# Layer 1's two attentions: negated scaled queries, softmax by head, grouped latent norms and another background plan

## The chip, the core and the metric

The kernel runs on one core of one Trainium2 chip. The metric is the time of one execution on the device, in microseconds (us), as the median of some runs. One profiled execution of the kernel before gives the trace that is read here. Its engines are named as in the profile: PE is TensorE's matmul, PEld its loading of weights, DVE is VectorE, ACT is ScalarE, POOL is GpSimd and SP is SyncE, which issues the DMAs.

## What is computed

A trunk of two transformer layers over 512 tokens (an 8 x 64 grid) with 256 context tokens beside them, 1024 features, all in float32. Layer 0 mixes with a pooling and a grouped attention; layer 1 with two attentions whose outputs are joined: MLA (8 heads, queries and keys from latents, 96 features a head, over all 768 keys) and a neighbourhood attention (8 heads of 64 features, 8 x 16 windows of the grid with a bias, and the 256 context keys). Each layer ends with a SwiGLU. Cut to the part that matters:

```python
def rmsnorm(x, g):
    xf = x.astype(jnp.float32)
    y = xf * lax.rsqrt(jnp.mean(xf * xf, axis=-1, keepdims=True) + EPS)
    return y.astype(x.dtype) * g

...
    def mla_q(cq_, T):
        q_ = (rmsnorm(cq_, q_a_gain) @ w_uq).reshape(B, T, MLA_HEADS, MLA_QK)
        return rmsnorm(q_, mla_q_gain)

    def mla_kv(ckv_, kr_, T):
        kv = (rmsnorm(ckv_, kv_a_gain) @ w_ukv).reshape(B, T, MLA_HEADS, MLA_NOPE + MLA_V)
        k_rope = jnp.broadcast_to(kr_[:, :, None, :], (B, T, MLA_HEADS, MLA_ROPE))
        k_ = jnp.concatenate([kv[..., :MLA_NOPE], k_rope], axis=-1)
        return rmsnorm(k_, mla_k_gain), kv[..., MLA_NOPE:]
    ...
    o_mla = block_attention(mq[:, :, :, None], jnp.concatenate([mkc, mk], axis=1),
                            jnp.concatenate([mvc, mv], axis=1), mla_scale).reshape(B, S, MLA_HEADS * MLA_V)
    ...
    na_scale = NA_HEAD_DIM ** -0.5
    o_na = neighbourhood_attention(q_na, k_na, v_na, k_nac, v_nac, na_rpb, na_scale).reshape(B, S, NA_DIM)

    out = jnp.concatenate([o_mla, o_na], axis=-1) @ w_out
```

## The kernel before

Activations are kept with features on the partitions and tokens along the free dimension. A float32 value is split into a high and a low part in the fp32r type (`H` and `L`), and a product is made of two or three matmuls (`mm3`, lines 133 to 137). Weights are loaded by SP into a staging buffer `wraw` (tag `wr`, four buffers), cast to `wH` on ACT (L123), and `wL` is the remainder, subtracted on DVE or POOL (L124).

The two attentions of layer 1 are 32 steps, driven by `paired`. First come 16 steps of window attention (`na_units`: 4 pairs of heads x 4 blocks of 128 queries), then 16 steps of MLA (`mla_units`: 4 pairs of heads x 4 blocks of queries). Each step has three parts. `scores` makes the scores in PSUM, the softmax's maximum on DVE (window: L1208 over the 256 context keys of both heads, then L1210, which adds the bias and takes the maximum over the window; MLA: L373), the bias `nb` of the exponential (L375), the exponential on ACT (L378), the reciprocal of its sum on DVE (L380) and the normalisation on POOL (L382). `turn` transposes the probabilities on PE (L389) into one of two PSUM buffers `ps_tp`, and copies them out on ACT (L165) or DVE (L167). `values` multiplies them with V (L1226, L1266). A step's `turn` runs one step after its scores, its `values` two steps after. Of a window step, all of `turn` comes at the end of the next step; of an MLA step two of its three transposes come right after the next scores.

Between them runs the background: the latents' queries, keys and values for MLA, which the plans `na_plan` and `mla_plan` deal out to the 32 steps. A `make` is a matmul of a latent with its weights into PSUM, a copy and a square on ACT (L1087, L1088), a sum on DVE (L1091) and then the inverse square root `rsqrt` without a table: eleven DVE instructions on 4 or 8 columns (L238, L244, and three times L247, L248, L249). Products with it follow: for queries on DVE (L1138, L1139), a rotation on POOL (L318 to L320) and its sum (L322); for keys on DVE (L1109) and POOL (L1111). A background `turn` (`turn_pair`, L1080) transposes two heads into a `ps_tp` buffer and splits them out, alternately on ACT (L344, `mQH`, `mKH`) and DVE (L345, `mQL`, `mKL`). The `make` of a value copies from PSUM on ACT (L1156). Keys that are made wait for their turns in staging buffers of the weights (tag `wr`), three for each of two groups of heads.

PE's order is written out: `block` in `paired` puts each part behind PE's last instruction. The order of the other engines' queues is chosen by the framework's scheduler, which may also bring loads forward as far as buffers allow. Each engine runs its queue in order.

## Time and profile before

| | us |
|---|---|
| median of three runs | 1744.32 (1743.94 to 1746.56) |
| the profiled execution | 1746.14 |
| its span in the trace | 1744.3 |
| PE busy | 1660.2 (95%) |
| DVE busy | 948.5 (54%) |
| ACT busy | 637.1 (37%) |
| POOL busy | 260.0 (15%) |

The span runs from the first to the last instruction that the profiler saw. A busy time is a sum over stages that have different limits, and the ends of PE's matmuls are modelled, so its 95% does not say that nothing can be won; what stops the kernel is read stage by stage. The span's stretches are named by us from its start. A wait is named by what ended it, an inference from semaphores.

### The profile page before, as it was taken

To read this page: it belongs to the slowest core of one execution; us is meant where nothing else is said; L and a number is where in the kernel's file an instruction comes from. 1 tells how busy PE (TensorE), PEld (TensorE's weight loads), DVE (VectorE), ACT (ScalarE), POOL (GpSimd) and SP (SyncE) were. 2 spreads that over 40 slices of the span, in tenths; PEclk is the share of its full clock that TensorE was granted. 3 is DMA by queue.
4 is the path that set the end of the run, shared out by engine and by line. 5 is a ranking of instruction groups with operands and counts; after the bars stand their busy time and mean duration, and the time that the engine had idled before them with its cause. 6 is when DMAs were issued, how large, how long until landed. Compare 5 with 4: busy or idle time off the path is not lost.

```text
span 1744.3 us, 29055 instructions
## 1 busy us (share of the span) xinstructions
PE 1660.2 (95%) x11662; PEld 1475.7 (85%) x11662; DVE 948.5 (54%) x2052; ACT 637.1 (37%) x1241; POOL 260.0 (15%) x406
## 2 busy tenths in 40 slices
PE   6898999999999999999999999879789999999999
PEld 3687777798888888888889999768678998999897
DVE  5687667555945434523327973867665543333332
ACT  4453556534211221121224643555554432232231
POOL 1441333110000000000001202645330100000000
PEclk8899999999999999999999999989999999999999
DMA  8311334301625414512213213210203032222221
GB/s 286 149 34 53 145 131 173 133 26 65 208 96 187 151 55 153 167 61 67 73 61 110 76 50 96 73 36 28 83 13 134 34 112 98 85 97 97 97 76 58
DMA packets 61527, 171.25 MB, mean 98 GB/s; under 512 B 7248, under 2 KB 15440, under 8 KB 61392
## 3 DMA queue, kind: packets, MB, share of 16 engines
q1 hardware_dynamic: 61392, 169.39, 28.8%
q8 instruction: 92, 1.51, 0.3%
q14 instruction: 43, 0.35, 0.1%
HBM read 160.05 MB, written 4.19 MB: 94 GB/s over the span
## 4 chain that ended last, share of the span: by engine, by line
PE 84%; DVE 8%; ACT 3%; DMA 2%; issue 1%; POOL 1%; SPq 0%; ACTq 0%; DVEq 0%; POOLq 0%
PE ps_one L135 17%; PE ps_one L136 17%; PE ps_one L137 17%; PE ps_tp L137 5%; PE ps_tp L135 5%; PE ps_tp L136 5%; PE ps_tp L389 3%; PE ps_pv L777 2%; ACT prob L378 1%; PE ps_pv L135 1%; PE ps_pv L137 1%; PE ps_pv L136 1%; PE ps_big L135 1%; PE ps_big L137 1%; PE ps_big L136 1%
## 5 line engine op out<-in xcount | busy, mean ns | idle before, releaser
L123 ACT CAST wH<-wraw 128x1024 fp32r<-128x1024 f32 (+5 forms) x215 | 195.0, 915 | 404.9 <-PE ps_one L136 199.4
L124 DVE TENSOR_TENSOR wL<-wraw,wH 128x1024 fp32r<-128x1024 f32 (+3 forms) x191 | 219.6, 1155 | 169.4 <-ACT wH L123 167.2
L137 PE MATMUL ps_one<-hH,wL 128*128 128x512 f32 (+1 forms) x704 | 236.8, 336 | 0.0
L136 PE MATMUL ps_one<-hL,wH 128*128 128x512 f32 (+1 forms) x704 | 236.8, 336 | 0.0
L135 PE MATMUL ps_one<-hH,wH 128*128 128x512 f32 (+1 forms) x704 | 236.7, 336 | 0.0
L137 PE MATMUL ps_tp<-hH,wL 128*128 128x256 f32 x704 | 196.6, 280 | 0.0
L136 PE MATMUL ps_tp<-hL,wH 128*128 128x256 f32 x704 | 196.3, 279 | 0.0
L135 PE MATMUL ps_tp<-hH,wH 128*128 128x256 f32 x704 | 196.0, 280 | 0.0
L137 PE MATMUL ps_one<-aH,wL 128*128 128x512 f32 (+1 forms) x560 | 194.0, 347 | 0.0
L136 PE MATMUL ps_one<-aL,wH 128*128 128x512 f32 (+1 forms) x560 | 193.9, 347 | 0.0
L135 PE MATMUL ps_one<-aH,wH 128*128 128x512 f32 (+1 forms) x560 | 193.5, 347 | 0.0
L289 POOL TENSOR_SCALAR hH<-nt 128x256 fp32r<-128x256 f32 (+1 forms) x72 | 39.5, 557 | 735.3 <-ACT nt L288 733.3
L137 PEld LDWEIGHTS ps_one<-hH,wL 128*128 128x128 f32 x704 | 132.2, 188 | 15.4
L136 PEld LDWEIGHTS ps_one<-hL,wH 128*128 128x128 f32 x704 | 132.2, 188 | 14.4
L135 PEld LDWEIGHTS ps_one<-hH,wH 128*128 128x128 f32 x704 | 132.3, 188 | 14.1
L382 POOL TENSOR_SCALAR prob<-prob,rs 128x768 f32<-128x768 f32 (+2 forms) x136 | 107.2, 798 | 198.4 <-DVE rs L380 136.3
L135 PEld LDWEIGHTS ps_tp<-hH,wH 128*128 128x128 f32 x704 | 132.3, 188 | 0.9
L136 PEld LDWEIGHTS ps_tp<-hL,wH 128*128 128x128 f32 x704 | 132.0, 188 | 1.0
L137 PEld LDWEIGHTS ps_tp<-hH,wL 128*128 128x128 f32 x704 | 132.3, 188 | 0.1
L389 PE MATMUL ps_tp<-ident,prob 128*128 128x128 f32 x656 | 98.9, 285 | 22.4 <-DVE mQL L345 5.9
L135 PEld LDWEIGHTS ps_one<-aH,wH 128*128 128x128 f32 x560 | 105.8, 189 | 14.7
L136 PEld LDWEIGHTS ps_one<-aL,wH 128*128 128x128 f32 x560 | 105.6, 189 | 14.6
(303 smaller groups left out, 3541.8 us busy)
## 6 DMA issues: line engine op xcount, KB each, us to landing
wraw<-in_ada_dram SPq DMA_DIRECT2D x80, 512.0 KB, 3.8
wraw<-in_wg_dram SPq DMA_DIRECT2D x44, 512.0 KB, 3.5
wraw<-in_wu_dram SPq DMA_DIRECT2D x44, 512.0 KB, 3.5
wraw<-in_wd_dram SPq DMA_DIRECT2D x32, 384.0 KB, 3.0
wraw<-in_wd_dram SPq DMA_DIRECT2D x16, 512.0 KB, 3.5
wraw<-in_w1n_dram SPq DMA_DIRECT2D x12, 512.0 KB, 3.5
adaw<-in_adaq_dram SPq DMA_DIRECT2D x16, 256.0 KB, 5.4
wraw<-in_adaq_dram SPq DMA_DIRECT2D x8, 512.0 KB, 6.2
```

The lines of the kernel that those rows point to most:

```text
L123: act.copy(H, raw[:, :cols])
L124: eng.tensor_tensor(L, raw[:, :cols], H.bitcast(F32), op=ALU.subtract)
L135: pe.matmul(o, aH, bH, start=first, stop=False)
L136: pe.matmul(o, aH, bL, start=False, stop=False)
L137: return pe.matmul(o, aL, bH, start=False, stop=last)
L289: last = (pool.tensor_scalar(H, t[:, :n], 1.0, 1.0, op0=ALU.mult, op1=ALU.mult), sub(L, t[:, :n], H))
L378: act.activation(pr[i], S[:, i, :], AF.Exp, bias=nb[:, i:i + 1], scale=scale, accum_out=sm[:, i:i + 1])
L382: pool.tensor_scalar(pr[i], pr[i], r[:, i:i + 1], 1.0, op0=ALU.mult, op1=ALU.mult)
L389: pe.transpose(tp[:, 128 * i:128 * i + 128], b, ident)
L777: pe.matmul(st["pv"][64 * hd:64 * hd + 64, tq], V[kt][:, 64 * kv:64 * kv + 64], pt[:, hd, kt - k0, :], start=kt == k0, stop=kt == 5)
```

## The change

Six things, all in layer 1's attentions.

1. The gains of the queries are multiplied by minus the softmax's scale (`neg`, two DVE instructions), so the scores come out scaled and negated. The row's minimum is then the exponential's bias as it stands: `softmax_of_negated` computes exp(mn - S) and has no L375. The window's bias is multiplied by -1 instead of by 8 on POOL.
2. In the window attention each head has its own minimum, exponential, reciprocal and normalisation, right behind its own four matmuls, the context keys first. Before, L1208, L375 and L380 were made for both heads at once.
3. All copies of the window's transposed probabilities go to ACT; before, two of three did.
4. The inverse square roots of the latents' norms are grouped: one for the four tiles of a pair of query heads (8 columns) instead of two of 4 columns, one for the six tiles of a group of key heads (24 columns) instead of three of 8. The products that follow go with it.
5. In a window step, background transposes are put right behind the scores, ahead of the values and of the makes.
6. The plan deals the background out anew: a step has a pair of lists, transposes and makes. The queries of the last two pairs of heads and the second group of keys move by one to three steps, loads of their weights by up to four.

```diff
     def rsqrt(r, src, scale, table=True):
         n = r.shape[-1]
-        m = small.tile([P, 8], F32, tag="nwm", name="nwm")[:, :n]
-        t = small.tile([P, 8], F32, tag="nwt", name="nwt")[:, :n]
+        width, tag, bufs = (8, "", 8) if n <= 8 else (24, "k", 1)
+        m = small.tile([P, width], F32, tag="nwm" + tag, name="nwm", bufs=bufs)[:, :n]
+        t = small.tile([P, width], F32, tag="nwt" + tag, name="nwt", bufs=bufs)[:, :n]
...
+    def softmax_of_negated(S, pr, mn):
+        sm = small.tile([P, 2], F32, tag="sm", name="sm")
+        act.activation(pr, S, AF.Exp, bias=mn, scale=-1.0, accum_out=sm[:, 0:1])
+        r = small.tile([P, 2], F32, tag="rs", name="rs")
+        dve.reciprocal(r[:, 0:1], sm[:, 0:1])
+        pool.tensor_scalar(pr, pr, r[:, 0:1], 1.0, op0=ALU.mult, op1=ALU.mult)
...
             early = turned[3] if turned else 0
+            turns, makes = unit[4] if unit and unit[4] else ((), ())
+            if not early:
+                for f in turns:
+                    block(f)
             for f in turned[1][:early] if turned else ():
                 block(f)
             if valued:
                 block(valued[2])
             background()
-            for f in unit[4] if unit else ():
+            for f in (*turns, *makes) if early else makes:
                 block(f)
...
+    neg = lp.tile([P, 2], F32, tag="neg", name="neg")
+    dve.tensor_scalar(neg[:, 0:1], gcol["nqg"], -0.125, None, op0=ALU.mult)
+    dve.tensor_scalar(neg[:, 1:2], gcol["mqg"], -(96 ** -0.5), None, op0=ALU.mult)
...
-    def tile_rstd(o, hv, extra=None):
-        nh = hv.shape[2]
+    def squares(o, hv, ss):
         act.copy(o, hv)
         act.square(hv, hv)
-        ss = small.tile([P, 8], F32, tag="ss", name="ss")[:, :2 * nh]
...
-        rsqrt(r, ss, 1.0 / 96, False)
+        dve.reduce_sum(ss, hv, axis=AX)
...
     def key_steps(g, w):
...
+        def norm():
+            dve.tensor_tensor(st["s"], st["s"], bc(krss, [P, 6, 4], 2), op=ALU.add)
+            r = small.tile([P, 24], F32, tag="rk", name="rk", bufs=1)
+            rsqrt(r, st["s"].rearrange("p t h -> p (t h)"), 1.0 / 96, False)
+            r = r.rearrange("p (t h) -> p t h", h=4)
+            for t0 in (0, 2, 4):
+                o = st[t0]
+                dve.tensor_tensor(o[..., 0:64], o[..., 0:64], bc(r[:, t0:t0 + 2], [P, 2, 4, 64], 3), op=ALU.mult)
+                for i in range(2):
+                    pool.tensor_tensor(o[:, i, :, 64:96], bc(krr[:, t0 + i, :], [P, 4, 32], 1),
+                                       bc(r[:, t0 + i], [P, 4, 32], 2), op=ALU.mult)
...
     def query_steps(pr, w):
...
+        def norm():
+            o = st["o"]
+            r = small.tile([P, 8], F32, tag="rq", name="rq")
+            rsqrt(r, st["s"], 1.0 / 96, False)
+            r = r.rearrange("p (t h) -> p t h", t=4)
...
-                pool.tensor_scalar(bias[hd, b], bias[hd, b], 8.0, 1.0, op0=ALU.mult, op1=ALU.mult)
+                pool.tensor_scalar(bias[hd, b], bias[hd, b], -1.0, 1.0, op0=ALU.mult, op1=ALU.mult)
...
                 for hd in range(2):
                     (QH, QL), K = (QQ[pr], QB)[hd], (KA, KB)[hd][pr]
-                    for so, ko in ((slice(0, 256), wk), (slice(256, 512), CTX)):
+                    for so, ko in ((slice(256, 512), CTX), (slice(0, 256), wk)):
...
-                dve.reduce_max(mc, S[:, :, 256:512], axis=AX)
-                for hd in range(2):
-                    dve.tensor_tensor_reduce(S[:, hd, 0:256], S[:, hd, 0:256], bias[hd, b], op0=ALU.add, op1=ALU.max, scale=1.0,
-                                             scalar=mc[:, hd:hd + 1], accum_out=mx[:, hd:hd + 1])
-                softmax(S, 2, 512, 0.125, st["p"], mx)
+                    mc = small.tile([P, 2], F32, tag="mc", name="mc")
+                    mn = small.tile([P, 2], F32, tag="mx", name="mx")
+                    dve.tensor_reduce(mc[:, 0:1], S[:, hd, 256:512], axis=AX, op=ALU.min)
+                    dve.tensor_tensor_reduce(S[:, hd, 0:256], S[:, hd, 0:256], bias[hd, b], op0=ALU.add, op1=ALU.min,
+                                             scale=1.0, scalar=mc[:, 0:1], accum_out=mn[:, 0:1])
+                    softmax_of_negated(S[:, hd], st["p"][hd], mn[:, 0:1])
...
-                transposed([st["p"][hd][:, 128 * j:128 * j + 128] for j in range(4)], st["t"][:, 4 * hd:4 * hd + 4, :], 2, 3)
+                transposed([st["p"][hd][:, 128 * j:128 * j + 128] for j in range(4)], st["t"][:, 4 * hd:4 * hd + 4, :], 1, 1)
...
-                    softmax(S[:, :TT].unsqueeze(1), 1, TT, 96 ** -0.5, [st["p"][hd]])
+                    mn = small.tile([P, 2], F32, tag="mx", name="mx")
+                    dve.tensor_reduce(mn[:, 0:1], S[:, :TT], axis=AX, op=ALU.min)
+                    softmax_of_negated(S[:, :TT], st["p"][hd], mn[:, 0:1])
...
-    turns0, turns1 = keys0[1], keys1[1]
-    (qa, ta, qb, tb), (qc, td, qd, te) = q[0], q[1]
-    na_plan = [keys0[0][:1], keys0[0][1:2], keys0[0][2:], [qa], [qb, hq[1]], [], [ta], [tb, qc], [qd], turns0[0][:1],
-               turns0[0][1:2] + [td], turns0[0][2:] + [v0], [te, hq[2]], vals0[:1], vals0[1:2], vals0[2:]]
-    (qa, ta, qb, tb), (qc, td, qd, te) = q[2], q[3]
-    mla_plan = [turns0[1][:1] + [qa], turns0[1][1:2] + [qb], turns0[1][2:] + [k1], [ta, keys1[0][0]], [tb, keys1[0][1]],
-                keys1[0][2:] + [v1], turns1[0][:1], turns1[0][1:] + turns1[1][:1] + [hq[3]], turns1[1][1:] + vals1[:1] + [qc],
-                vals1[1:] + [qd], [], [td, te], [], [], [], []]
+    (ka, kb, kc), kn, (kt, ku) = keys0
+    (qa, qb), qn0, qt = q[0]
+    (qc, qd), qn1, qu = q[1]
+    na_plan = [((), (ka,)), ((), (kb,)), ((), (kc, kn)), ((), (qa,)), ((), (qb, qn0, hq[1])), ((), ()),
+               (qt[:1], (qc,)), (qt[1:], (qd, qn1)), ((), (v0,)), (kt[:1], ()), ((kt[1], qu[0]), ()), (kt[2:], ()),
+               (qu[1:], (vals0[0],)), ((), (vals0[1], hq[2])), ((), (vals0[2], k1)), ((), ())]
+    (ka, kb, kc), kn, (kt, kv) = keys1
+    (qa, qb), qn0, qt = q[2]
+    (qc, qd), qn1, qu = q[3]
+    mla_plan = [(ku[:1], (qa,)), (ku[1:2], (ka,)), (ku[2:], (qb, qn0)), ((), (kb,)), ((), (kc, kn, hq[3], v1)), (qt[:1], ()),
+                ((qt[1], kt[0]), (qc,)), (kt[1:], (qd, qn1)), (kv[:1], (vals1[0],)), (kv[1:2], vals1[1:]),
+                ((kv[2], qu[0]), ()), (qu[1:], ()), (), (), (), ()]
```

In the plans `ka`, `kb`, `kc` are the makes of keys, `qa` to `qd` of queries, `kn` and `qn` the norms, `kt`, `ku`, `kv`, `qt`, `qu` the transposes; `hq`, `k1`, `v0`, `v1` load weights.

## Rows read from the trace of the kernel before

**Rows 1.** Windows: us; busy us of PE, PEld, DVE, ACT, POOL; clock; DMA.

```profile
1088.30:1183.20 94.90, 75.84 (x647) 67.12 (x645) 68.43 (x241) 52.56 (x132) 53.08 (x94) 0.91 0.19 50
1183.20:1286.80 103.60, 86.51 (x755) 75.80 (x753) 77.09 (x222) 55.95 (x128) 43.71 (x65) 0.97 0.16 52
1286.80:1303.90 17.10, 17.10 (x147) 14.96 (x145) 10.58 (x23) 7.89 (x16) 3.63 (x4) 0.87 0.00 1
```

**Rows 2.** Chain that ended last, shares by line: 1088.3 to 1183.2, then 1183.2 to 1286.8.

```profile
by line: PE ps_tp L389 10.0%; ACT prob L378 8.6%; PE ps_pv L1226 8.1%; DMA wraw<-in_wuq_dram 6.8%; DVE ps_big L1210 6.0%; issue 5.9%; PE ps_big L1207 5.6%; PE ps_big L1206 5.5%; DVE mc L1208 4.3%; PE ps_pv L135 3.3%; DVE PT L167 2.7%; ACT P
...
by line: DVE mx L373 12.7%; ACT prob L378 6.3%; DVE rq L249 5.9%; DMA wraw<-in_w1o_dram 5.4%; DVE PT L167 5.4%; issue 5.3%; PE ps_tp L389 4.0%; DVE nwt L248 3.9%; DVE nwt L247 3.8%; PE ps_pv L135 3.7%; DMA wraw<-in_wuq_dram 3.7%; PE ps_pv L
```

**Rows 3.** Lines of DVE, 1088.3 to 1326: count, busy us, mean ns, idle before.

```profile
L373 DVE TENSOR_REDUCE mx<-ps_big 128x1 f32<-128x768 f32 x32 | 30.1, 950 | 5.4 <-PE ps_big L137 5.1
L167 DVE COPY PT<-ps_tp 128x512 f32<-128x512 f32 x35 | 23.9, 684 | 8.9 <-PE ps_tp L389 8.9
L1210 DVE CUSTOM_DVE_ANT_0 ps_big<-ps_big,bias,mc 128x256 f32<-128x256 f32 x32 | 16.2, 505 | 0.8 <-DVE mc L1208 0.2
L1208 DVE TENSOR_REDUCE mc<-ps_big 128x2 f32<-128x512 f32 x16 | 11.0, 688 | 6.3 <-PE ps_big L1207 6.2
L249 DVE SCALAR_TENSOR_TENSOR rq<-nwt,rq 128x4 f32<-128x4 f32 (+1 forms) x42 | 10.7, 259 | 0.9
L248 DVE TENSOR_TENSOR nwt<-nwt,nwm 128x4 f32<-128x4 f32 (+1 forms) x42 | 8.8, 214 | 0.8
...
L247 DVE SCALAR_TENSOR_TENSOR nwt<-rq 128x4 f32<-128x4 f32 (+1 forms) x42 | 8.4, 203 | 0.5
L375 DVE TENSOR_SCALAR nb<-mx 128x1 f32<-128x1 f32 (+1 forms) x48 | 8.2, 174 | 0.3
L380 DVE RECIPROCAL rs<-sm 128x1 f32<-128x1 f32 (+1 forms) x48 | 7.7, 162 | 21.9 <-ACT prob L378 21.4
...
L1210 DVE DVE_READ_ACCUMULATOR2_ANT mx<- 128x1 f32 x32 | 4.5, 141 | 0.0
L238 DVE TENSOR_SCALAR nwm<-ss 128x4 f32<-128x4 f32 (+1 forms) x14 | 3.9, 275 | 0.0
L244 DVE TENSOR_SCALAR rq<-nwm 128x4 int32<-128x4 int32 (+1 forms) x14 | 3.5, 249 | 0.1
```

**Rows 4.** Lines by form of ACT and of POOL, 1088.3 to 1326.

```profile
L165 ACT COPY PT<-ps_tp 128x512 f32<-128x512 f32 x45 | 26.1, 588 | 36.4 <-PE ps_tp L389 36.4
L378 ACT ACTIVATE prob<-ps_big,nb 128x512 f32<-128x512 f32 x32 | 21.7, 683 | 15.4 <-DVE nb L375 7.2 <-DVE nwt L248 4.3 <-DVE rq L249 3.6
...
L382 POOL TENSOR_SCALAR prob<-prob,rs 128x512 f32<-128x512 f32 x32 | 22.4, 711 | 21.2 <-DVE rs L380 11.8 <-DVE rq L249 3.1 <-DVE nwt L248 3.1
```

**Rows 5.** Waits of PE, 1088.3 to 1183.2: us in total, times, longest.

```profile
PE ps_tp L389 <- DVE mKL L345: 3.4, 1, 3.4
...
PE ps_tp L389 <- DVE mQL L345: 1.3, 1, 1.3
```

**Rows 6.** Waits of PE, 1183.2 to 1286.8.

```profile
PE ps_tp L389 <- DVE mQL L345: 4.6, 2, 3.4
PE ps_pv L135 <- ACT mV L1156: 4.0, 1, 4.0
```

**Rows 7.** Chain in order of time, 1236 to 1256: start us, us, what.

```profile
1238.79 3.83 DMA wraw<-in_wuq_dram
```

**Rows 8.** Timeline of DVE, then of POOL, about 1236: start us, us, instruction.

```profile
1236.09 0.77 DVE L249 SCALAR_TENSOR_TENSOR rq<-nwt,rq 128x8 f32<-128x8 f32 x1
...
1235.90 0.95 POOL L382 TENSOR_SCALAR prob<-prob,rs 128x768 f32<-128x768 f32 x1 [0.94 <-DVE nwt L247]
```

**Rows 9.** Lines L247, L1109, L1111, 1088.3 to 1326: ns min/median/max.

```profile
L247 DVE SCALAR_TENSOR_TENSOR nwt<-rq x42: 144/162/747, 1096.9 to 1277.6; 128x4 f32<-128x4 f32 x24, 128x8 f32<-128x8 f32 x18
...
L1109 DVE TENSOR_TENSOR kr<-kr,rq x6: 671/766/918, 1101.4 to 1239.5; 128x512 f32<-128x512 f32 x6
...
L1111 POOL TENSOR_TENSOR kr<-krr,rq x12: 392/398/902, 1101.5 to 1239.1; 128x128 f32<-128x128 f32 x12
```

More of the change, by code (lines that the diff above doesn't have):

```diff
@@ L980, in turn @@
                         for pr in range(2):
-                            sink(2 * half + pr, slice(128 * t0, 128 * t0 + 256), tp[:, pr, :], gcol[gain])
+                            sink(2 * half + pr, slice(128 * t0, 128 * t0 + 256), tp[:, pr, :], qgain[gain])
                     later(turn)
@@ L1082, in turn_pair @@
             split_out(dst[a][0][:96, sl], dst[a][1][:96, sl], tp[:96, a], g[:96])
-    def tile_rstd(o, hv, extra=None):
-        nh = hv.shape[2]
+    def squares(o, hv, ss):
         act.copy(o, hv)
         act.square(hv, hv)
-        ss = small.tile([P, 8], F32, tag="ss", name="ss")[:, :2 * nh]
-        sv = ss.rearrange("p (t h) -> p t h", t=2)
-        dve.reduce_sum(sv, hv, axis=AX)
-        if extra is not None:
-            dve.tensor_tensor(sv, sv, bc(extra, [P, 2, nh], 2), op=ALU.add)
-        r = small.tile([P, 8], F32, tag="rq", name="rq")[:, :2 * nh]
-        rsqrt(r, ss, 1.0 / 96, False)
-        return r.rearrange("p (t h) -> p t h", t=2)
+        dve.reduce_sum(ss, hv, axis=AX)
     def key_steps(g, w):
@@ L1105, in make @@
                 tok_gemm(pt[:, i, :], w(), 1, 256, lk[t0 + i])
+            if t0 == 0:
+                st["s"] = small.tile([P, 6, 4], F32, tag="ssk", name="ssk", bufs=1)
             o = st[t0] = wrp.tile([P, 1024], F32, tag="wr", name="kr")[:, :768].rearrange("p (t h d) -> p t h d", t=2, h=4)
[L1107 to L1112 removed]
+            squares(o[..., 0:64], pt.rearrange("p t (h d) -> p t h d", d=64), st["s"][:, t0:t0 + 2])
+        def norm():
[9 more added lines that the diff above has]
+                                       bc(r[:, t0 + i], [P, 4, 32], 2), op=ALU.mult)
         def turn(t0, h2):
@@ L1119, in turn @@
             turn_pair(t0, st[t0][:, :, 2 * h2:2 * h2 + 2], gcol["mkg"], mK[at:at + 2])
-        return ([lambda t0=t0: make(t0) for t0 in (0, 2, 4)],
+        return ([lambda t0=t0: make(t0) for t0 in (0, 2, 4)], norm,
                 [[lambda t0=t0, h2=h2: turn(t0, h2) for t0 in (0, 2, 4)] for h2 in range(2)])
@@ L1132, in make @@
                 tok_gemm(pt[:, i, :192], w(), 1, 192, lq[t0 + i])
-            o = st[t0] = wp.tile([P, 2, 2, 96], F32, tag="qr", name="qr", bufs=3)
-            hv = pt[:, :, :192].rearrange("p t (h d) -> p t h d", d=96)
-            r = tile_rstd(o, hv)
-            qn = wp.tile([P, 2, 2, 32], F32, tag="qn", name="qn", bufs=1)
-            tmp = wp.tile([P, 2, 2, 32], F32, tag="rt", name="rt", bufs=1)
-            dve.tensor_tensor(qn, o[..., 64:96], bc(r, [P, 2, 2, 32], 3), op=ALU.mult)
-            dve.tensor_tensor(o[..., 0:64], o[..., 0:64], bc(r, [P, 2, 2, 64], 3), op=ALU.mult)
-            C, S = (bc(tabs["q", i][:, t0:t0 + 2, :], [P, 2, 2, 32], 2) for i in range(2))
+            if t0 == 0:
+                o = slot3(F32, "qr") if pr == 1 else wp.tile([P, TT], F32, tag="qr", name="qr", bufs=1)
+                st["o"] = o.rearrange("p (t h d) -> p t h d", t=4, h=2)
+                st["s"] = small.tile([P, 8], F32, tag="ss", name="ss")
+            squares(st["o"][:, t0:t0 + 2], pt[:, :, :192].rearrange("p t (h d) -> p t h d", d=96),
+                    st["s"][:, 2 * t0:2 * t0 + 4].rearrange("p (t h) -> p t h", t=2))
+        def norm():
[3 more added lines that the diff above has]
+            r = r.rearrange("p (t h) -> p t h", t=4)
+            qn = wp.tile([P, 4, 2, 32], F32, tag="qn", name="qn", bufs=1)
+            tmp = wp.tile([P, 4, 2, 32], F32, tag="rt", name="rt", bufs=1)
+            dve.tensor_tensor(qn, o[..., 64:96], bc(r, [P, 4, 2, 32], 3), op=ALU.mult)
+            dve.tensor_tensor(o[..., 0:64], o[..., 0:64], bc(r, [P, 4, 2, 64], 3), op=ALU.mult)
+            C, S = (bc(tabs["q", i], [P, 4, 2, 32], 2) for i in range(2))
             rope(o[..., 64:96], qn, C, S, 16, tmp, now=True)
@@ L1145, in turn @@
                 mQ[2 * pr:2 * pr + 2] = [padded(group_pair(0, "mQ") if pr < 2 else mQx[2 * pr - 4 + i]) for i in range(2)]
-            turn_pair(t0, st[t0], gcol["mqg"], mQ[2 * pr:2 * pr + 2])
-        return [f for t0 in (0, 2) for f in ((lambda t0=t0: make(t0)), (lambda t0=t0: turn(t0)))]
+            turn_pair(t0, st["o"][:, t0:t0 + 2], neg[:, 1:2], mQ[2 * pr:2 * pr + 2])
+        return ([lambda t0=t0: make(t0) for t0 in (0, 2)], norm, [lambda t0=t0: turn(t0) for t0 in (0, 2)])
     def value_steps(g, w):
```

9 lines of the change are left out of this document (1 added, 8 removed).

## The prediction, made before the result was known

> **What bounds the kernel now.** I read the stretches first. The change touches only layer 1's two attentions (and two tiny instructions ahead of them), which run from 1088.3 us, the first window score, to about 1326. The first 16 steps, the window attention, take 94.9 us and TensorE is busy in 75.8 of them; the next 12, the first three quarters of MLA, take 103.6 with 86.5; the next 17.1 us, which hold three MLA steps without background work, have TensorE busy throughout [rows 1]. So an MLA step alone is bound by TensorE at some 5.7 us, and what there is to win lies in the first two stretches: 19.1 + 17.1 = 36.2 us of idle TensorE. No other engine is full: VectorE is busy in 68.4 and 77.1 us, ScalarE in about 55 each. These are waits in a chain, so I read the chain next [rows 2]. In the window stretch it alternates between TensorE, the two steps of the maximum (L1208 and L1210), the exponentials and one weight load. In the MLA stretch the maximum (12.7%) leads, the Newton lines L247 to L249 together have 13.6%, and two weight loads have 9.1%. VectorE runs its queue in order, so a chain of eleven tiny Newton instructions stands ahead of the maxima and reciprocals that TensorE's next transposes need. Then come the prices of the instructions [rows 3, 4].
>
> **The change part by part.**
> *A, grouped norms.* Fourteen inverse square roots (8 of query makes, 6 of key makes) become six. Lines L249, L248, L247, L238 and L244 are busy 35.3 us in this stage [rows 3], 2.5 us for each of the fourteen; eight fewer free 20 us of VectorE. Wider operands (8 and 24 columns instead of 4 and 8) cost little: a Newton instruction alone lasts some 0.16 us [rows 9]. What of this is on the path? In the MLA stretch the three Newton lines have 13.6% of 103.6 = 14.1 us of the chain, and seven chains there become three: 14.1 x 4/7 = 8.1. In the window stretch no Newton line is among those shown, the last shown having 2.7% = 2.6 us; three such lines would be at most 7.8, of which 4/7 is 4.4. I take 2, bounds 0 and 4.4.
>
> *B, softmax by head in the window attention.* Now the exponential of head 0 waits for a reduction over both heads (0.69), two passes of 0.51 with an accumulator read of 0.14 each, and the bias multiplication (0.17): 2.2 us [rows 3]. Then both exponentials (2 x 0.68), one reciprocal (0.16) and two products on GpSimd (2 x 0.71) follow before head 1 is ready: 5.1 us from the end of the scores [rows 3, 4]. After, each head has its own 256-wide minimum. None is in the trace; the reductions of 512 and 768 elements (0.69, 0.95) lie on a line of 1.02 ns an element, which gives 0.43. Head 0 needs 0.43 + 0.51 + 0.14 = 1.08 and starts while TensorE still does head 1; head 1 needs 2 x 1.08, then 0.68 + 0.16 + 0.71 = 3.7. That is 1.4 us sooner per step. L1208 has 4.3% = 4.1 us of the chain, that is 6 of its 16 instructions, so 6 x 1.4 = 8.4 if each counts in full. The value matmuls that stand between hide a part: I take 7, bounds 0 and 8.4.
>
> *C, negation.* The 48 bias multiplications (8.2 us) vanish. In the window stretch B has counted them. In MLA, L373 has 12.7% = 13.2 us of the chain, that is 14 instructions of 0.95, each followed by one such multiplication: 14 x 0.17 = 2.4. I take 2. The minimum is priced like the maximum, as the trace has no minimum. If the form of L1210 needed one more pass of 0.51 for each of its 32, that would be 16 us of VectorE, of which VectorE's share of the chain (some third) would show: +5 as the upper bound, 0 taken.
>
> *D, copies of the window's transposes.* All 32 now go to ScalarE: 11 of 0.68 leave VectorE and add 11 x 0.59 = 6.5 us to ScalarE [rows 3, 4], which has some 40 us idle in that stretch [rows 1]. The chain holds 2.6 us of the VectorE copies [rows 2]. Taken 0, bounds -2.6 (they leave the chain) and +6.5 (each new one is late).
>
> *E, order and plan.* In window steps the background's transposes now come right behind the scores, so that the value matmuls cover the evacuation of their PSUM buffer. TensorE waited 3.4 + 1.3 us there for mKL and mQL [rows 5]; I take 2, bounds 0 and 4.7. In MLA the like wait for mQL (4.6) [rows 6] is VectorE's lateness, which A holds. The last query weights (hq[3]) are asked for three steps earlier: one load of 3.8 us on the chain [rows 7] was theirs. The other pieces are w1o loads, 5.4% [rows 2], behind which the copies that end TensorE's 4.0 us wait for mV [rows 6] stood on ScalarE. Those loads are not moved. I take 3.8, bounds 0 and 9.4, the whole 9.1% [rows 2]. The other weights move by up to four steps either way; every load leaves SP in order, needs a staging buffer that a GpSimd subtraction frees and a ScalarE cast in order; key tiles hold three of the four staging buffers, before and after, so moved loads pass the same SP, ScalarE and GpSimd queues.
>
> *F, what is added.* Sixteen more reductions (16 x (2 x 0.43 - 0.69) = 2.7 us) and sixteen more reciprocals (2.6 us) on VectorE [rows 3]. Of these 5.3 us a third, its chain share, shows: +2, bounds 0 and 5.3. The two instructions for the negated gains lie in a stretch where TensorE has other work: 0, at most 0.4.
>
> One row asks for care. The Newton instruction at 1236.09 took 0.77 us, not 0.16, and ended with a GpSimd product that ran from 1235.90 for 0.95 [rows 8, 9]. So a two-input VectorE instruction in SBUF can stand still beside GpSimd. The Trainium skill (SBUF — State Buffer, SBUF: two separate sides) calls the port pair the two share an exclusive lock, held for a whole instruction; by that rule, this trace agrees. It speaks for A as eight chains fewer, and against it for the keys: the grouped step has three VectorE products and six GpSimd products in one place. Their rows show 0.67 to 0.92 and 0.39 to 0.90 [rows 9]: in single file 3 x 0.67 + 6 x 0.39 = 4.4 us, in which no probabilities are normalised. If all of it lands on the path, twice, it is +8.8; the turns that need these keys come two steps later at the earliest, so I take 0 and keep +8.8 as a rival.
>
> The sum: -8.1 - 2 - 7 - 2 - 2 - 3.8 + 2 = -22.9. That leaves some 13 of the 36 us of idle TensorE, so TensorE is not yet what stops it. The profiled execution took 1746.1 us (span 1744.3, the rest lies outside it), 1.8 above the median of the three runs, 1744.3. So 1746.1 - 22.9 = 1723.2, less 1.8: 1721.4, and I say 1722.
>
> **The rivals.**
> *TensorE everywhere.* If the freed VectorE also takes the waits that A to E leave, all bounds on the good side: 8.1 + 4.4 + 8.4 + 2.4 + 2.6 + 4.7 + 9.4 = 40: 1704. The granted clock was 0.91, 0.97 and 0.87 of 2.4 GHz in the three stretches, each a mean of time at 2.4 and at 1.2 GHz [rows 1]; it was lowest in the densest stretch, so I count nothing for it. Against this rival: starts and ends of stretches can't be filled.
> *The key burst.* The grouped key step holds GpSimd and VectorE for 4.4 us twice, with the exponentials' products behind: 1722 + 8.8 = 1731.
> *Off the path.* The freed time was hidden, and the next thing late is the product on GpSimd or the load: 1744. For it: no engine is full, so that each wait has another just behind it. Against it: 13.6% of the chain in instructions that vanish by half.
> *Slower: ScalarE behind its loads.* Nineteen weight casts stand in ScalarE's queue in this stage, each after a load through one free staging buffer. In the window stretch no copy can pass them any more, since VectorE does none. Now 16 us of loads are on the chain (6.8% of 94.9 and 9.1% of 103.6) [rows 2]. At 3.8 us each [rows 7], all gain is gone when loads of 16 + 23 = 39 us, eleven of the nineteen, are waited for in full. If fourteen are, 53 us, it gives 1744.3 + 14 = 1758. For it: the order of every queue but TensorE's is chosen anew by the scheduler, and it placed casts ahead of late loads already.
> *That it does not do what it says* (the order of the queues leaves the maxima late although the Newton chains are fewer) falls into off the path.
>
> **How the numbers follow.** Forecast (1711 to 1735, around 1722) 0.53; TensorE everywhere (1700 to 1711) 0.10; the key burst and other half gains (up to 1740.8) 0.12; off the path 0.10; slower 0.15. A measurement of this kernel can tell 0.2%, 3.5 us, from no change: within that lie 1740.8 to 1747.8. So faster 0.75, same 0.10, slower 0.15. The range leaves out slower, and half of TensorE everywhere: 1706 to 1748.
>
> **What would show it.** A: Newton lines at 6/14 of their number and under 7% of the MLA stretch's chain; fewer GpSimd waits for them. B: the window reductions at about 0.43 and window steps near 5 us on average instead of 5.9. C: no L375 line in the stage. D: ScalarE under 65 us in the window stretch with TensorE's waits for its copies no longer than before. E: TensorE's waits for mKL and mQL in the window stretch gone. F: added VectorE lines of some 5 us. Wrong would be: window steps as long as before with ScalarE idle ahead of casts (slower), or TensorE's idle time in the two stretches not falling under 25 us (off the path).

## The result, and the profile after

The change makes the kernel slower: 1760.25 us (median; 1755.0 to 1769.78) against 1743.24 for the kernel before beside it (1739.29 to 1746.56), a ratio of 1.0101 with a 95% interval of 1.0077 to 1.0126. The forecast of 1722, with its range of 1711 to 1735, lies on the other side of no change.

The profiled execution has a span of 1756.8 us, 12.5 more than before. The windows of the kernel after, cut at the same events as [rows 1] (first window score, first MLA score, thirteenth MLA score, last score; columns as there):

```profile
1090.60:1208.60 118.00, 81.94 (x645) 71.66 (x644) 59.44 (x195) 60.19 (x144) 52.99 (x88) 0.87 0.15 40
1208.60:1303.60 95.00, 86.68 (x756) 76.99 (x754) 66.04 (x142) 56.47 (x127) 43.15 (x59) 0.96 0.18 57
1303.60:1318.80 15.20, 15.20 (x146) 13.20 (x145) 10.66 (x20) 8.98 (x19) 5.11 (x6) 1.00 0.01 2
```

The window stretch went from 94.9 to 118.0 us (+23.1), the first twelve MLA steps from 103.6 to 95.0 (-8.6), the next three from 17.1 to 15.2 (-1.9). The start lies 2.3 us later, and what follows the last score is 2.4 shorter (440.4 to 438.0): together the +12.5. So the loss sits in one place, and it hides a gain elsewhere. TensorE's waits in the window stretch name it (engine, tile and line, what it waited for; us in total, times, longest):

```profile
PE ps_big L1234 <- ACT prob L388: 33.8, 16, 2.8
PE ps_tp L398 <- ACT PT L165: 1.8, 2, 0.9
PE ps_tp L398 <- DVE mKL L346: 0.3, 1, 0.3
```

The first line has no counterpart before: there no score matmul waited in this stretch, and the largest line, ahead of those of [rows 5], was

```profile
PE ps_pv L1226 <- ACT PT L165: 4.6, 5, 2.0
```

Now one score matmul in each of the 16 steps waits for an exponential, 2.1 us a time. One such step in the timeline (start, us, engine, line, operation; in brackets the idle time before and what ended it):

```profile
1190.41 0.28 PE L1235 MATMUL ps_big<-nKA,nQL 128*128 128x256 f32 x1
1190.72 0.43 DVE L1238 TENSOR_REDUCE mc<-ps_big 128x1 f32<-128x256 f32 x1 [1.70 <-PE ps_big L1235]
1191.19 0.49 DVE L1239 CUSTOM_DVE_ANT_0 ps_big<-ps_big,bias,mc 128x256 f32<-128x256 f32 x1
1191.60 0.14 DVE L1239 DVE_READ_ACCUMULATOR2_ANT mx<- 128x1 f32 x1
1191.83 0.69 ACT L388 ACTIVATE prob<-ps_big,mx 128x512 f32<-128x512 f32 x1 [0.84 <-DVE mx L1239]
1192.66 0.39 PE L1234 MATMUL ps_big<-nKB,nQBH 128*128 128x256 f32 x1 [1.98 <-ACT prob L388]
```

`nKA` is head 0, `nKB` head 1. Both heads' scores lie in one PSUM tile, `S = ps_big([P, 2, 512])`. The change puts head 0's softmax ahead of head 1's matmuls in the program, and from then on head 1's write into its half of `S` stands behind the last reader of head 0's half. The softmax by head, meant to run beside TensorE, runs in series with it: TensorE stands still for reduction, bias, exponential, and only then makes head 1's scores. The readers are in order on other engines; TensorE, whose order is written out by hand, has its values, transposes and makes behind the waiting matmul.

Idle TensorE in that stretch rose from 94.90 - 75.84 = 19.1 to 118.00 - 81.94 = 36.1 us, that is 17.0 of the 23.1; the other 6.1 are the busy time of TensorE's own instructions, as many as before, at a granted clock of 0.87 instead of 0.91 of 2.4 GHz.

### The profile page after: what moved, and what is told of

The parts are those of the page before. It is cut to its first block, busy times and chain, and to the rows that moved or that the text cites. A ratio compares the mean times of both kernels' runs of the same rounds, so it can differ in the third digit from the quotient of the medians.

```text
span 1756.8 us, 28962 instructions
## 1 busy us (share of the span) xinstructions
PE 1665.8 (95%) x11662; PEld 1479.9 (84%) x11662; DVE 929.6 (53%) x1923; ACT 645.4 (37%) x1252; POOL 258.6 (15%) x394
## 4 chain that ended last, share of the span: by engine, by line
PE 88%; DVE 5%; ACT 3%; DMA 1%; issue 1%; POOL 1%; SPq 0%; ACTq 0%; DVEq 0%; POOLq 0%
PE ps_one L135 17%; PE ps_one L136 17%; PE ps_one L137 17%; PE ps_tp L137 5%; PE ps_tp L135 5%; PE ps_tp L136 5%; PE ps_tp L398 4%; PE ps_pv L791 2%; PE ps_pv L135 2%; PE ps_big L137 2%; PE ps_big L135 2%; PE ps_big L136 2%; PE ps_pv L137 2%; PE ps_pv L136 2%; PE ps_big L809 1%
## 5 line engine op out<-in xcount | busy, mean ns | idle before, releaser
L135 PEld LDWEIGHTS ps_one<-hH,wH 128*128 128x128 f32 x704 | 132.3, 188 | 14.1
L137 PEld LDWEIGHTS ps_one<-aH,wL 128*128 128x128 f32 x560 | 105.2, 188 | 14.6
L398 PE MATMUL ps_tp<-ident,prob 128*128 128x128 f32 x656 | 98.3, 284 | 10.3 <-ACT PT L165 3.6
```

Source lines behind the costliest of these rows:

```text
L135: pe.matmul(o, aH, bH, start=first, stop=False)
L137: return pe.matmul(o, aL, bH, start=False, stop=last)
L398: pe.transpose(tp[:, 128 * i:128 * i + 128], b, ident)
```

## The experiments

The theory: the shared tile's new dependence is the whole loss, and without it the forecast's 1722 holds. The rival: the loss comes from the softmax by head itself, or from the new plan. Each ratio is taken against the kernel before, timed beside the run (1743.89 us beside e1 to e4, 1742.53 beside e5 to e8, 1742.14 beside e9 to e12). "Window" and "MLA" are the stretches above (16 and 12 steps) in the one profiled execution, whose time stands in the column "profiled".

| | median us | ratio, 95% | profiled us | window | MLA |
|---|---|---|---|---|---|
| before | 1743.24 | 1 | 1746.14 | 94.9 | 103.6 |
| after | 1760.25 | 1.0101 (1.0077 to 1.0126) | 1758.70 | 118.0 | 95.0 |
| e1_scores_first | 1722.35 | 0.9869 (0.9849 to 0.9889) | 1728.37 | 87.6 | 95.3 |
| e2_before_by_head | 1788.18 | 1.0245 (1.0220 to 1.0271) | 1787.84 | 137.9 | 101.7 |
| e3_both_heads | 1731.76 | 0.9919 (0.9890 to 0.9949) | 1733.88 | 94.4 | 95.7 |
| e4_own_tiles | 1724.70 | 0.9887 (0.9866 to 0.9908) | 1725.29 | 88.1 | 94.6 |
| e5_turns_later | 1722.92 | 0.9890 (0.9867 to 0.9912) | 1723.25 | 87.3 | 95.0 |
| e6_turns_last | 1730.06 | 0.9937 (0.9913 to 0.9960) | 1732.99 | 95.1 | 92.6 |
| e7_norms_apart | 1722.02 | 0.9893 (0.9870 to 0.9915) | 1721.85 | 81.6 | 95.6 |
| e8_copies_shared | 1726.21 | 0.9908 (0.9881 to 0.9936) | 1730.17 | 92.5 | 93.4 |
| e9_old_plan | 1727.12 | 0.9912 (0.9898 to 0.9927) | 1726.62 | 82.7 | 98.3 |
| e10_bias_copy | 1732.79 | 0.9943 (0.9931 to 0.9955) | 1732.81 | 90.8 | 95.4 |
| e11_grouped_again | 1725.84 | 0.9893 (0.9875 to 0.9911) | 1726.71 | 87.2 | 94.8 |
| e12_apart_again | 1721.23 | 0.9878 (0.9864 to 0.9892) | 1720.52 | 82.9 | 94.8 |

Two pairs are the same kernel (e1 and e11, e7 and e12): a stretch repeats to 1.3 us, a median to 3.5. A stretch speaks for one execution only: those of e1, e6, e8 and e11 were the longest of their kernels, e1's 6.0 us above its median.

### The wait: e1, e2, e4

e1 changes the program's order alone: all score matmuls of a step, then the softmax of each head. The tile is the same.

```diff
                         pe.matmul(S[:, hd, so], QL[:, tq], K[:, ko], start=False, stop=True)
+                for hd in range(2):
                     mc = small.tile([P, 2], F32, tag="mc", name="mc")
```

> The changed kernel with one edit: the score matmuls of both heads of a window step are issued first, and the softmax by head follows. Theory (new wait: head 1's score matmuls wait for head 0's exponential, 33.8 us of idle TensorE in 16 steps): these waits vanish, the 16 window steps fall from 118 us to about 82, the time from 1760 to about 1722 (1714 to 1732). Rival (the window steps are long because ScalarE now makes all copies, or because of the plan): the steps stay above 110 us and the time above 1750.

Measured: 1722.35 us as expected, and a window stretch of 87.6, which is 5.6 above the 82 expected. TensorE's waits there no longer hold a score matmul; the longest is another, for the background:

```profile
PE ps_tp L1100 <- DVE rs L390: 5.9, 1, 5.9
PE ps_tp L398 <- ACT PT L165: 2.6, 2, 1.5
PE ps_tp L398 <- POOL prob L391: 2.1, 2, 1.5
PE ps_tp L398 <- DVE mKL L346: 1.7, 1, 1.7
```

e2 adds the suspected part alone to the kernel before, keeping its plan, norms and copies: the reductions, exponentials and products by head, each behind its own matmuls, with the context keys first as in the change.

```diff
-                dve.reduce_max(mc, S[:, :, 256:512], axis=AX)
-                for hd in range(2):
...
+                    dve.reduce_max(mc[:, 0:1], S[:, hd, 256:512], axis=AX)
...
-                softmax(S, 2, 512, 0.125, st["p"], mx)
+                    softmax(S[:, hd:hd + 1, :], 1, 512, 0.125, st["p"][hd:hd + 1], mx)
```

> The kernel before with one part of the change alone: in a window step each head has its own scores, maximum, bias, exponential, reciprocal and product, right behind its own matmuls; all else as before. Theory (new wait): head 1's matmuls wait for head 0's exponential here too, 16 waits of about 2.1 us, and the time rises by 25 to 35 us to 1768 to 1778. Rival (plan or copies): the time stays within 5 us of 1743.

Measured: 1788.18 us, more than the 1768 to 1778 expected, and the same wait at the head of the window stretch's list:

```profile
PE ps_big L1204 <- ACT prob L378: 38.3, 16, 3.0
```

e4 keeps the order of the change, head by head, and gives each head a tile of its own, half the size: four of them in place of two of `S`. For that it also opens the pool of PSUM tiles anew ahead of the window attention and behind it (`banks`).

```diff
-                S = ps_big([P, 2, 512])
                 for hd in range(2):
+                    S = ps.tile([P, 1, 512], F32, tag="half", name="ps_half", bufs=4)
...
-                        pe.matmul(S[:, hd, so], QH[:, tq], K[:, ko], start=True, stop=False)
+                        pe.matmul(S[:, 0, so], QH[:, tq], K[:, ko], start=True, stop=False)
...
+        banks(4)
...
+        banks(5)
```

> The changed kernel with one edit: each head's scores have a PSUM tile of their own (four tiles of one bank in place of two of two banks), in the changed order, head by head. Theory (the wait is one for the shared tile, not for data): no wait of head 1's matmuls for head 0's exponential, the time as with scores first, 1714 to 1732. Rival (what is waited for is something else, as a place in a queue): above 1750.

Measured: 1724.70 us, like e1. Its waits name the new tile once, ahead of the first score:

```profile
PE ps_tp L1100 <- DVE qr L323: 5.7, 1, 5.7
PE ps_tp L398 <- ACT PT L165: 3.8, 2, 2.2
PE ps_tp L398 <- DVE mKL L346: 2.1, 1, 2.1
PE ps_half L1234 <- ACT mV L165: 1.2, 1, 1.2
```

So two edits that have nothing else in common, one of order and one of tiles, each remove the wait and some 36 to 38 us, and a third brings it into the kernel before. The cause is shown. The halves of `S` don't overlap, head 1 reads nothing of head 0: the dependence belongs to the tile, not to the data. The Trainium skill (Perfetto Trace Analysis, Matmuls) says that independent matmul groups should rotate through different PSUM banks, so that one group's evacuation overlaps the next group's matmuls. Here that is not enough: the two heads' groups lie in different halves of `S`, one bank each as e4's text counts them, and waited 2.1 us a step; the overlap came with e4's separate tiles, or with e1's order.

### What the softmax by head is worth: e3

e3 is the change with one minimum, one reciprocal and two exponentials for both heads behind all scores, as before; everything else new.

```diff
-                    dve.tensor_reduce(mc[:, 0:1], S[:, hd, 256:512], axis=AX, op=ALU.min)
...
+                dve.tensor_reduce(mc, S[:, :, 256:512], axis=AX, op=ALU.min)
...
+                dve.reciprocal(r, sm)
```

> The changed kernel with the window softmax over both heads at once again (one minimum over both, one reciprocal, all score matmuls first); negation, grouped norms, order, plan and copies stay changed. Theory (new wait): the window steps return to 95 us or less and the MLA steps keep their gain of 8 to 13 us: 1722 to 1735, above the run with scores first by what the softmax by head is worth (0 to 8 us). Rival: above 1750.

Measured: 1731.76 us. The window stretches of e1, then e3:

```profile
1090.08:1177.72 87.64, 72.67 (x647) 64.31 (x645) 55.73 (x193) 58.04 (x142) 52.16 (x87) 0.94 0.21 55
1089.19:1183.54 94.35, 77.39 (x647) 69.82 (x645) 54.37 (x163) 57.41 (x141) 51.37 (x86) 0.87 0.19 51
```

Once off TensorE's way, the softmax by head is worth 6.7 us there; the prediction had 7. Only 2.0 of them are idle time of TensorE (15.0 against 17.0 us), the waits that the prediction counted; 4.7 are the same 647 matmuls at a granted clock of 0.94 instead of 0.87. That the softmax by head is what raised the clock is not shown.

### The grouped norms: e5, e7, e11, e12

In e1 the wait of 5.9 us stands in the seventh window step, which lasts 13.87 us. What ended it, in the timeline (the profile names a reciprocal as releaser; the turn reads `qr`, whose last writer, L323, ends at 1127.61):

```profile
1120.78 0.15 DVE L250 SCALAR_TENSOR_TENSOR rq<-nwt,rq 128x8 f32<-128x8 f32 x1
...
1123.10 0.42 DVE L1168 TENSOR_TENSOR qn<-qr,rq 128x256 f32<-128x256 f32 x1
1123.44 0.68 DVE L1169 TENSOR_TENSOR qr<-qr,rq 128x512 f32<-128x512 f32 x1
1125.54 0.45 POOL L320 TENSOR_TENSOR rt<-qn,tab1q 128x128 f32<-128x128 f32 x1
1125.95 0.71 POOL L321 TENSOR_TENSOR qr<-qn,tab1q 128x256 f32<-128x256 f32 x1
1126.70 0.91 DVE L323 TENSOR_TENSOR qr<-qr,rt 128x256 f32<-128x256 f32 x1 [1.59 <-POOL qr L321]
1127.76 1.06 PE L1100 MATMUL ps_tp<-ident,qr 128*96 128x128 f32 x4 [5.93 <-DVE rs L390]
```

One chain now serves four tiles of queries, so none of the four is ready before all are, and the turn, put right behind the scores, stands first in TensorE's queue.

e5 is e1 with the two turns of these queries one step later:

```diff
-               (qt[:1], (qc,)), (qt[1:], (qd, qn1)), ((), (v0,)), (kt[:1], ()), ((kt[1], qu[0]), ()), (kt[2:], ()),
+               ((), (qc,)), (qt[:1], (qd, qn1)), (qt[1:], (v0,)), (kt[:1], ()), ((kt[1], qu[0]), ()), (kt[2:], ()),
```

> The kernel of e1 (1722.4 us) with the two background transposes of the first pair's queries one window step later (steps 7 and 8 instead of 6 and 7). In e1's profile the turn in step 6 stood at the head of TensorE's queue for 5.93 us, waiting for the grouped query norm's products and rotation, which began in step 4. Theory (an order set by hand too early costs its wait in full): the wait goes or falls under 1 us, the window stretch goes from 87.6 to about 83, and the time to about 1717. Rival (the same chain stops the next step instead, since the queries' norm holds VectorE and GpSimd anyway): the wait turns up at another line of steps 6 to 8, and the time stays within 1721 to 1724.

Measured: 1722.92 us, window 87.3: the theory of its text fell. The wait is gone, but its time is not:

```profile
PE ps_tp L398 <- ACT PT L165: 4.1, 3, 2.2
PE ps_pv L1256 <- ACT PT L165: 2.5, 3, 1.5
PE ps_tp L398 <- POOL prob L391: 2.1, 2, 1.5
```

The seventh step fell from 13.87 to 7.77 us, and the five behind it rose from 24.62 in sum to 30.76.

e7 gives each make its own inverse square root again, 14 chains instead of 6, and leaves all else as in e1. Of the queries:

```diff
-                st["s"] = small.tile([P, 8], F32, tag="ss", name="ss")
...
+            ss = small.tile([P, 8], F32, tag="ss", name="ss")[:, :4]
...
+            r = small.tile([P, 8], F32, tag="rq", name="rq")[:, :4]
+            rsqrt(r, ss, 1.0 / 96, False)
```

> The kernel of e1 (1722.4 us) with the change's edit 4 undone: each make has its own inverse square root again, 14 chains of VectorE instructions instead of 6; plan, order and softmax as in e1. The prediction's part A took 8.1 us in the MLA stretch and 2 in the window stretch: if it holds, about 1732, most of it in the MLA stretch, with the Newton lines back in its chain. Rival (the grouped norm's delay of the keys and queries takes back what fewer chains give, in the window stretch above all): the MLA stretch longer by 4 to 8, the window stretch shorter by 4 to 6, the time 1720 to 1726.

Measured: 1722.02 us, window 81.6, MLA 95.6. The window stretch is as the rival had it, 6.0 shorter; the MLA stretch is not longer, against both. Beside one another on one chip, e1 and e7 once more:

> The kernel of e1 once more, beside e7's on the same chip, since the two were timed apart from each other. In their profiles the grouping of the norms cost 6.0 us in the window stretch (87.6 against 81.6) and won 0.3 in the MLA stretch. If that stands: this kernel is some 5 us slower than e12. If the prediction's part A stands (10 us won): some 10 us faster. If the two cancel in most executions: within 2 us.

> The kernel of e7 once more, beside e1's on the same chip: scores of both heads first, then softmax by head; each make with its own inverse square root; all else as in the change. Expected at 1717 to 1722, about 1.3% under the kernel before, the fastest of all if the profiles' stretches stand.

Measured: 1725.84 us grouped (1720.05 to 1726.71), 1721.23 apart (1720.37 to 1723.12). The ranges overlap, so the medians alone settle no more than that the grouping doesn't win 10 us. The windows of the two (first two lines e11, then e12) show where their profiled executions differ:

```profile
1089.57:1176.77 87.20, 72.80 (x646) 64.54 (x645) 55.22 (x193) 58.20 (x142) 52.35 (x87) 0.94 0.21 55
1176.77:1271.61 94.84, 87.02 (x756) 77.08 (x754) 66.55 (x145) 57.34 (x127) 43.52 (x60) 0.96 0.18 57
```

```profile
1087.73:1170.61 82.88, 72.07 (x647) 64.13 (x645) 62.57 (x245) 57.52 (x142) 54.04 (x93) 0.96 0.22 58
1170.61:1265.44 94.83, 83.89 (x756) 74.10 (x753) 77.42 (x197) 56.64 (x127) 44.79 (x66) 1.00 0.18 57
```

Grouping costs 4.3 us in the window stretch (6.0 in the first pair) and nothing either way in MLA (94.84 and 94.83; -0.3 in the first pair), though it frees VectorE of 7.4 and 10.9 us there. The other grouped kernels without the shared tile's wait have 88.1 (e4) and 87.3 (e5) in the window stretch, and e9, apart, has 82.7, so the cost there is no chance of one execution. How much of it reaches the median is less clear: 0.3 us in the first pair, which was not timed side by side, 4.6 in the second.

### Place of the turns, copies, plan, negation: e6, e8, e9, e10

e6 is e1 with the background transposes behind the values again, as before.

```diff
-            if not early:
-                for f in turns:
-                    block(f)
...
-            for f in (*turns, *makes) if early else makes:
+            for f in (*turns, *makes):
```

> The kernel of e1 (1722.4 us) with the change's edit 5 undone: in a window step background transposes come behind the values again, just ahead of the makes, not behind the scores. The prediction's part E took 2 us for that edit. If it holds: about 1724 to 1725, and TensorE's waits for mKL and mQL come back. If, as e1's profile suggests, the place behind the scores is what makes step 6 wait 5.9 us for the query norm, the values now cover some of that wait, and the time falls to about 1718 to 1720. If both: within 1 us of e1.

Measured: 1730.06 us, outside what was expected either way, window 95.1 (+7.5), MLA 92.6 (-2.7). Of the 2.7, 2.0 are TensorE's busy time at a granted clock of 0.98 instead of e1's 0.96; e7 and e12, one kernel, had 0.98 and 1.00 there, so this is not shown to be the edit's. The new place wins more than the 2 us taken, and not by the waits that the prediction named: mKL has 2.2 us in e6 and 1.7 in e1; the first line is what grew (2.1 in e1):

```profile
PE ps_tp L398 <- POOL prob L391: 6.3, 5, 2.7
PE ps_tp L1097 <- DVE rs L390: 4.9, 1, 4.9
```

With the turns ahead, TensorE has work while GpSimd still makes the products for its next transposes.

e8 is e1 with VectorE making one copy in three of the window's transposed probabilities again:

```diff
-                transposed([st["p"][hd][:, 128 * j:128 * j + 128] for j in range(4)], st["t"][:, 4 * hd:4 * hd + 4, :], 1, 1)
+                transposed([st["p"][hd][:, 128 * j:128 * j + 128] for j in range(4)], st["t"][:, 4 * hd:4 * hd + 4, :], 2, 3)
```

> The kernel of e1 (1722.4 us) with the change's edit 3 undone: one third of the copies of the window's transposed probabilities goes to VectorE again, 11 of 32. The prediction's part D took 0, with bounds: the edit wins up to 2.6 us or loses up to 6.5. If 0 holds: 1721 to 1724, and nothing in the waits for those copies. If the edit won by taking copies out of VectorE's queue: up to 1725. If ScalarE's queue, with its casts behind loads, made the copies late: down to 1716.

Measured: 1726.21 us, window 92.5 (+4.9), MLA 93.4 (-1.9). The 1.9 lie in the clock alone: idle TensorE is 8.1 us in both, busy 85.3 at 0.98 against 87.2 at 0.96. In the window stretch TensorE now waits for the copies that were moved:

```profile
PE ps_pv L1256 <- DVE PT L167: 2.7, 1, 2.7
PE ps_tp L398 <- DVE PT L167: 2.3, 1, 2.3
```

The intervals of e8 and e1 touch, so the loss rests on the window stretch and these two lines.

e9 is e7 with the background dealt out to the steps as in the kernel before:

```diff
...
-    mla_plan = [(ku[:1], (qa,)), (ku[1:2], (ka,)), (ku[2:], (qb, qn0)), ((), (kb,)), ((), (kc, kn, hq[3], v1)), (qt[:1], ()),
+    mla_plan = [(ku[:1], (qa,)), (ku[1:2], (qb, qn0)), (ku[2:], (k1,)), (qt[:1], (ka,)), (qt[1:], (kb,)),
+                 ((), (kc, kn, v1)), (kt[:1], ()), ((kt[1], kt[2], kv[0]), (hq[3],)), (kv[1:], (vals1[0], qc)),
...
```

> The kernel of e7 (scores of both heads first, norms apart) with the background dealt out to the 32 steps as in the kernel before (edit 6 undone); the place of the turns, softmax by head, negation and copies stay new. The MLA stretch was 103.6 us before and 95.6 in e7, though e7 has all 14 Newton chains: something other than the grouping won its 8 us. Theory (the plan did): the MLA stretch goes back to 101 to 104 us and the time to about 1728. Rival (the negation did, which takes a VectorE instruction out from between each minimum and its exponential): the MLA stretch stays at 95 to 97, and the time within 1720 to 1724.

Measured: 1727.12 us (1725.74 to 1729.15) beside 1721.23 (1720.37 to 1723.12) of e12. The MLA stretch is 3.5 us longer than in e12, 2.8 than in e7: between the 101 to 104 us of the theory and the 95 to 97 of the rival. In the profiles another 2.6 us lie ahead of the first window score, where e7 and e12, one kernel, differ by 1.7. The MLA stretch of e9:

```profile
1172.97:1271.30 98.33, 87.49 (x756) 76.36 (x754) 76.40 (x196) 57.61 (x130) 44.11 (x64) 0.97 0.17 55
```

e10 is e7 with the multiplication of each minimum put back, by 1, ahead of its exponential:

```diff
+        nb = small.tile([P, 2], F32, tag="nb", name="nb")
+        dve.tensor_scalar(nb[:, 0:1], mn, 1.0, None, op0=ALU.mult)
...
-        act.activation(pr, S, AF.Exp, bias=mn, scale=-1.0, accum_out=sm[:, 0:1])
+        act.activation(pr, S, AF.Exp, bias=nb[:, 0:1], scale=-1.0, accum_out=sm[:, 0:1])
```

> The kernel of e7 with the 48 to 64 small VectorE multiplications put back that the negation removed: each minimum is multiplied by 1 into a tile of its own, from which the exponential takes its bias, once for each head. Plan, order and all else as in e7. The prediction's part C took 2 us in MLA, and the window's share lay in part B. If 2 to 4 us holds: 1724 to 1726, some 0.17 us for each of the 24 to 28 minima on the path, so the MLA stretch 97 to 98. If the negation won the 8 us of the MLA stretch: it goes to 102 or more, and the time to 1729 or more. If it is hidden: within 1 us of e7 in both stretches.

Measured: 1732.79 us beside 1721.23; window 90.8 (+7.9 on e12), MLA 95.4 (+0.6 on e12, -0.1 on e7). None of the three expectations: MLA doesn't move, the window stretch does. Its last step has 9.85 us instead of 3.45, in which TensorE waits once, for a product on GpSimd:

```profile
PE ps_tp L400 <- POOL prob L393: 6.3, 1, 6.3
```

That engine's queue and the reciprocals that release the products, in the timeline:

```profile
1173.13 0.16 DVE L392 RECIPROCAL rs<-sm 128x1 f32<-128x1 f32 x1
1174.86 0.16 DVE L392 RECIPROCAL rs<-sm 128x1 f32<-128x1 f32 x1 [0.93 <-ACT prob L390]
1175.45 2.77 POOL L1089 MEMSET mKx<- 32x768 f32 x4
1177.02 0.16 DVE L392 RECIPROCAL rs<-sm 128x1 f32<-128x1 f32 x1 [0.91 <-ACT prob L390]
1178.17 0.52 POOL L1089 MEMSET mQH<- 32x512 f32 x1
...
1179.71 0.69 POOL L393 TENSOR_SCALAR prob<-prob,rs 128x512 f32<-128x512 f32 x1
```

Zeros for the padding of later keys and queries went ahead of products that were ready: the one at 1179.71 had its reciprocal at 1173.29. In e12 the same zeros come one product later, behind that of 1167.47, and TensorE does not wait for them. So 6.4 of the 7.9 us are an order of GpSimd's queue that the small edit tipped over; 1.5 is left, net of steps that gained and steps that lost, for the multiplications themselves.

## Why the prediction was wrong

**The step that failed** is in part B: "Head 0 needs 0.43 + 0.51 + 0.14 = 1.08 and starts while TensorE still does head 1". The first half was right: L1238 took 0.42 us on average (0.43 forecast), and the step shown has 0.43 + 0.49 + 0.14 = 1.06. The second half was never read from anything. The diff shows both heads in one `S`, and the order of the program makes head 1's write follow head 0's reads. The prediction followed the dependences of the data and not those of the tile. Part B was thus an added wait, 2.1 us in each of 16 steps. What had to be asked is what the instruction next on TensorE, head 1's first matmul, is waiting for after the edit. No row of before could have shown this wait, because in that order TensorE has written both halves of `S` before anything reads it.

**The rival on the slow side** was another mechanism. It had ScalarE's casts behind late loads; after the change ScalarE is busy 60.2 of 118.0 us, under the 65 forecast, and 1.8 us of TensorE's waits for its copies in the window stretch are less than the 6.1 before. e1 settles it: it keeps every load and cast of the change and takes 1722.35 us. That the rival's 1758 lies 2 us from the 1760.25 measured is luck. Part D's sign was wrong on the good side: 0 taken with at most 2.6 won, 4.9 in the window stretch (e8).

**Part A**, the largest term, was wrong as well, hidden behind B. VectorE's work was sized rightly: the five Newton lines fell from 35.3 us [rows 3] to 17, 18 of the 20 forecast. Of after, VectorE by line (instructions, then busy us, mean ns; these are the 8-column forms of three lines, the 24-column forms and the other two lines make up the rest of the 17):

```profile
L250 DVE SCALAR_TENSOR_TENSOR rq<-nwt,rq 128x8 f32<-128x8 f32 x12 | 4.2, 349 | 0.4
L248 DVE SCALAR_TENSOR_TENSOR nwt<-rq 128x8 f32<-128x8 f32 x12 | 3.2, 264 | 0.2
L249 DVE TENSOR_TENSOR nwt<-nwt,nwm 128x8 f32<-128x8 f32 x12 | 2.5, 212 | 0.3
```

And in the MLA stretch's chain the Newton lines fell from 13.6% to some 4%, under the 7% that A's own sign asked for. The largest shares by line, after, and then of e12, which has all 14 chains:

```profile
by line: PE ps_tp L398 10.5%; PE ps_pv L1297 7.7%; DVE mx L1282 6.5%; PE ps_big L137 5.8%; PE ps_big L136 5.7%; PE ps_big L135 5.6%; PE ps_pv L135 5.3%; DMA wraw<-in_w1o_dram 4.8%; PE ps_pv L137 4.6%; PE ps_pv L136 4.5%; POOL prob L391 4.1%
```

```profile
by line: DVE mx L1282 14.7%; DVE PT L167 6.5%; DVE rq L250 5.8%; issue 5.8%; DVE nwt L248 5.3%; DVE nwt L249 4.8%; DMA wraw<-in_w1o_dram 4.3%; DVE ss L1108 3.6%; PE ps_tp L398 3.2%; PE ps_pv L1297 3.1%; DVE mKL L346 2.6%; DVE rq L245 2.3%; 
```

Two chains as different as that, and the stretches are 95.0 and 94.8 us. The step that failed is "14.1 x 4/7 = 8.1": a share of the chain was taken for a saving. An explanation that fits, though no run shows it by itself: where VectorE's queue and TensorE's run almost level, the chain only says by which of the two it was followed back; the other is as long. TensorE's idle time did fall, from 94.83 - 83.89 = 10.9 (e12) to 94.84 - 87.02 = 7.8 us (e11), 3.1 where 8.1 were forecast; but the same 756 matmuls took 3.1 us more at a granted clock of 0.96 instead of 1.00. The first pair has the same in small: 1.9 us less idle in e1 than in e7, 1.7 more busy at 0.96 instead of 0.98. Whether the lower clock comes with the grouping is open. In the window stretch the grouping costs 4 to 6 us. That a chain which serves four tiles makes the first of them late is seen in e1's wait of 5.9 us; since e5 took that wait away and won nothing, how the rest of the cost arises is open. The prediction weighed such a delay for keys only (the key burst); that one is there too, small: the seventh MLA step lasts 12.90 us in e1 and 10.35 in e7.

**Part B's own size** came out, 6.7 (e3) for 7, but in part by luck: 2.0 of it are waits, the rest is the granted clock. **Part C** took 2 in MLA; e10 shows 0.6 at most. **Part E**: the turns' place won 7.5 in the window stretch for 2 taken, and not through [rows 5] only; the plan won 2.8 to 3.5 in MLA (e9) for 3.8 taken. The wait of 4.6 us for mQL [rows 6], which E left to A, is 0.5 in e7 with all fourteen chains, so it goes without A. **Part F** was as sized (32 reductions of 421 ns are 13.5 us, 2.5 more than before; 2.7 forecast); its part on the path wasn't tested.

So had the shared tile been seen and avoided, 1722 would have been met (e1: 1722.35), but by other terms. A, 10.1 in the forecast, wins nothing: by the medians the grouping is 0.3 and 4.6 us behind. D and E, 5.8 together in the forecast, are worth 4.9, 7.5 and some 3 us in the stretch that each moved. And 4.3 came behind the two stretches, where nothing was forecast; 1.9 of them are three MLA steps that are TensorE's alone, at a granted clock of 1.00 instead of 0.87. A right sum of wrong terms is no right prediction. What is left open: of the 8.6 us that MLA gained, the plan holds about 3, the negation under 1 and the grouping none. With the old plan and all chains (e9) the stretch is still 5.3 under before; the wait for `mV` of [rows 6], 4.0 us, is 0.7 in e9, but which edit moved the copies ahead of it was not tried.

The best version is the change with e1's order and the norms apart (e12, 1721.23 us, 1.2% under the kernel before); e1, e4 and e5 can't be told from it by their intervals.

## What to carry to other kernels

When an edit lets a reader of one half of a buffer start early, look up which tile the next writer of the other half writes, and in what order the program names them: put all writes ahead of the first read, or give each half its own tile. A share of the chain bounds a gain and is none by itself; before it is booked, ask how much shorter the other engine's queue is in the same stretch. Grouping small instructions saves their engine's time and delays the first of the group, so count who waits for that one.
